# A state product in three rounded products, with the step size moved into an exponent

## The chip, the cores and the metric

The kernel runs on one core of a Trainium2 chip. A core has a matrix engine (TensorE, in the profile PE, with its weight loads as PEld), a vector engine (VectorE, DVE), an engine for functions of one variable (ScalarE, ACT), a general one (GpSimd, POOL) and a queue that issues transfers (SyncE, SP). TensorE reads SBUF and writes PSUM, a small memory of eight banks. DVE and ACT reach both; POOL and the transfers reach SBUF only. The metric is the device time of one execution in microseconds (us).

## The reference, cut to what matters

The kernel computes one layer of a decoder: a pooling branch and a state-space branch (SSD) run on the same 1024 prompt rows and 64 sample rows, are gated, added and projected. The change lies in the SSD of the prompt rows, which go in 8 chunks of 128 rows, for 4 groups of 8 heads (head width 64, state width 128):

```python
acs = jnp.cumsum(dq * Ag, axis=1)
seg = acs[:, :, None] - acs[:, None, :]
decay = jnp.exp(jnp.where(mask, seg, -jnp.inf))
cb = jnp.einsum('bign,bjgn->bijg', Cq, Bq)
att = cb[..., None] * decay * dq[:, None]
y = jnp.einsum('bijge,bjgep->bigep', att, xq)
y = y + jnp.einsum('bign,bige,bgepn->bigep', Cq, jnp.exp(acs), h)
last = acs[:, -1]
w_in = jnp.exp(last[:, None] - acs) * dq
h = h * jnp.exp(last)[..., None, None] + jnp.einsum('bjgn,bjge,bjgep->bgepn', Bq, w_in, xq)
```

Here `dq` is dt, the step size of each row and head. It enters twice: in `att`, which weights the rows of x inside a chunk, and in `w_in`, which weights them on their way into the state `h` that goes from chunk to chunk.

## The kernel before

The kernel is written as Python generators that a scheduler turns into one instruction stream for each engine. Its order of engines' work comes from the order in the program and from a simulated timeline. In the chunk stage the order on PE and on SP is fixed to that of the program (`ORDER`, L1838, applied by `in_line`, L1873); on ACT, DVE and POOL the scheduler chooses it beforehand, and each engine then takes its instructions strictly one after another.

Products in fp32 run in the full type, or split: a matrix is rounded to the shorter type F32R (`hi`), the rest is kept (`lo`), and three products hi·hi, lo·hi and hi·lo are added in PSUM. The large matrices (`gemm_`, L353, line L358) are done so.

Before the chunk stage, `dt_end` (from L1082) makes for all chunks dt (`dtT`), the cumulated decays (`acT`), the weights into the state (`wdT`) and a copy of the decays in DRAM (`acs_d`), from which each chunk loads its own, spread over the partitions.

The chunk stage runs 32 generators `chunk(g, c)` (L1495), 8 chunks in each of 4 groups, staggered in a loop (L1849 to L1868). One of them goes through these steps:

- A: loads of the decays `dec`, of B and C (`bc`) and of x (`xb`);
- B: `cE` = exp(-decay) on ACT; then `far` on POOL (L1198) masks the upper half of `dec`, and `exps` (L1207) makes eight exponentials on ACT, one for each head, with `acT` as bias;
- C: PE transposes x to `px` (L1516) and B to `pbc` (L1518) and makes C·B beside it (L1519). ACT copies the transposed B out (`bt`, L1521) and C in (L1523). DVE makes `xd` = x·dt (L1527) and `xw` = x·w_in (L1529), both out of `px`, and multiplies `dec` and `cE` (L1534, L1536);
- D: PE makes the state product `pu` (L1541), one product in full fp32 of 128 by 128 by 512, and the inner products (`inner`, L1219 and L1222); POOL and DVE update the state `hst` (L1547, L1549), DVE adds the skip term (L1554);
- E: `finish` (L1474 to L1485) gates, splits and squares the result; after the last chunk of a group PE turns the state for its output (L1561).

In iteration i of the loop stand step C of chunk i+1, then filler, then D of chunk i, the loads and exponentials of chunks i+3 and i+2, E of chunk i, and filler again. The filler (`products`, L1831) are pieces of the large projections, 2.56 of them for a chunk, each 12 products of 352 or 384 columns (L358); DVE or ACT takes each out (L1732, L1750, L1753). From chunk 10 on, `wo_splits` (L1779) also splits a weight matrix with work for DVE, ACT, POOL and both transfer queues.

`px`, `pbc`, the output of `inner` and the turned state are PSUM tiles of one kind, `ps` (`PB`, L97), four banks in turn. `pu` has one bank of its own (`PC`), the filler three (`PA`). `bt` and `xd` have two buffers, `xw` has one.

Of the kernel before, what the change touches and what calls it, by code (L numbers as in the profile page):

```python
# [8 lines left out]
F32 = mybir.dt.float32  # L9
F32R = mybir.dt.float32r  # L10
AF = mybir.ActivationFunctionType
ALU = mybir.AluOpType
# [8 lines left out]
P = 128  # L21
# [7 lines left out]
NH = 32  # L29
# [4 lines left out]
NC = SEQ // CH  # L34
# [12 lines left out]
def tile_pool_ssd_step(  # L47
# [9 lines left out]
    def nm(s):  # L57
        uid[0] += 1
        return f"{s}_{uid[0]}"
# [3 lines left out]
    sm = ctx.enter_context(tc.tile_pool(name="sm", bufs=2))  # L63
# [6 lines left out]
    def open_(name, bufs, side="left"):  # L70
        cm = tc.tile_pool(name=name, bufs=bufs, side=side, reuse_waits="tile")
        kept.append(cm)
        return cm.__enter__()
# [20 lines left out]
    def Y4(pool, dt=F32R):  # L94
        return pool.tile([P, 4, T], dt, tag="Y", name=nm("Y"), bufs=2)

    def PB():  # L97
        return psB.tile([P, 512], F32, tag="ps", name=nm("ps"))

    def PA():  # L100
        return psA.tile([P, 512], F32, tag="mm", name=nm("mm"))

    def PC():

        return psC.tile([P, 512], F32, tag="pc", name=nm("pc"))
# [6 lines left out]
    mm = nc.tensor.matmul  # L112
    act = nc.scalar.activation
    V = nc.vector
# [967 lines left out]
    def dt_end():  # L1082
# [87 lines left out]
        for c0 in range(0, 9, 4):  # L1170
# [10 lines left out]
            else:  # L1181
# [2 lines left out]
                act(E[:, :NS], at[:, :NS], AF.Exp, scale=-1.0)  # L1184
                store_(E_d, E[:, :NS])


    SSTEPS = 7

    def decays(dec, g, c):  # L1190

        S = P if c < NC else NS
        load(dec, acs_d[c, 8 * g:8 * g + 8, :S].partition_broadcast(S))

    def far(dec, c):

        if c < NC:
            nc.gpsimd.affine_select(dec, dec, [[0, 8], [1, P]], ALU.is_ge, FAR, base=0, channel_multiplier=-1)  # L1198
        else:
            dS = dec.rearrange("p h (b i) -> p h b i", i=8)  # L1200
            nc.gpsimd.affine_select(dS, dS, [[0, 8], [8, NB], [1, 8]], ALU.is_ge, FAR, base=0, channel_multiplier=-1)
            nc.gpsimd.affine_select(dS, dS, [[0, 8], [-8, NB], [0, 8]], ALU.is_ge, FAR, base=0, channel_multiplier=1)

    def exps(dec, g, c):
        S = P if c < NC else NS
        for h in range(8):
            act(dec[:, h], dec[:, h], AF.Exp, bias=acT[:S, c, 8 * g + h:8 * g + h + 1], scale=-1.0)  # L1207
# [6 lines left out]
    def inner(xd, dec, S, state=None, cE=None):  # L1214
        pi = PB()
        for q in range(4):
            o = [pi[64 * hh:64 * hh + 64, q * S:(q + 1) * S] for hh in range(2)]
            for hh in range(2):
                mm(o[hh], xd[:S, 2 * q + hh, :], dec[:S, 2 * q + hh], start=True, stop=state is None)  # L1219
            for hh in range(2 if state is not None else 0):  # L1220
                h = 2 * q + hh
                mm(o[hh], state[:, h * 64:h * 64 + 64], cE[:, h], start=False, stop=True)  # L1222
        return pi[:, :4 * S].rearrange("p (q i) -> p q i", i=S)
# [242 lines left out]

    CKL = ("sz", "v")

    def ckt(shape, tag, bufs=2):
        return (cl if tag in CKL else ca if tag in ("dec", "xb", "cE", "bc") else ck).tile(list(shape), F32, tag=tag, name=nm(tag), bufs=bufs)  # L1470

    def finish(g, o, S, v, sz):

        V.tensor_tensor(v, v, sz, ALU.mult)  # L1474
        yhc = yh[g][:, :, o:o + S]
        act(yhc, v, AF.Copy)  # L1476
        act(sz, v, AF.Square)
        nc.gpsimd.tensor_tensor(yl[g][:, :, o:o + S], v, yhc.bitcast(F32), ALU.subtract)  # L1478
        nc.gpsimd.tensor_tensor(sz[:, 0:2], sz[:, 0:2], sz[:, 2:4], ALU.add)
        sa = sq_acc[:, o:o + S]  # L1480
        if g == 0:
            nc.gpsimd.tensor_tensor(sa, sz[:, 0], sz[:, 1], ALU.add)
        else:
            nc.gpsimd.tensor_tensor(sz[:, 0], sz[:, 0], sz[:, 1], ALU.add)
            nc.gpsimd.tensor_tensor(sa, sa, sz[:, 0], ALU.add)  # L1485

    def sample_end(g):
        sz = ckt([P, 4, NS], "szs", 1)
        load(sz, z_d[g][:, :, SEQ:])
        v = ckt([P, 4, NS], "v", 1)  # L1490
        load(v, ys_d[g])
        yield
        finish(g, SEQ, NS, v, sz)

    def chunk(g, c):  # L1495
        o = c * P
        dec = ckt([P, 8, P], "dec", 3)
        decays(dec, g, c)
        bc = ckt([P, 2, P], "bc", 3)
        load(bc, xbc_d[g][:, 4:6, o:o + P])  # L1500
        Bf, Cf = bc[:, 0], bc[:, 1]
        xb = ckt([P, 4, P], "xb", 5)
        load(xb, xbc_d[g][:, 0:4, o:o + P])
        yield
        if c > 0:
            cE = ckt([P, 8, P], "cE")
            act(cE, dec, AF.Exp, scale=-1.0)
        if g > 0 or c > 0:
            far(dec, c)
            exps(dec, g, c)  # L1510
            yield
        sz = ckt([P, 4, P], "sz", 3)
        load(sz, z_d[g][:, :, o:o + P])
        px = PB()
        for q in range(4):
            nc.tensor.transpose(px[:, q * P:(q + 1) * P], xb[:, q], ident)  # L1516
        pbc = PB()
        nc.tensor.transpose(pbc[:, :P], Bf, ident)  # L1518
        mm(pbc[:, P:2 * P], Bf, Cf, start=True, stop=True)  # L1519
        bt = ckt([P, P], "bt", 2)  # L1520
        act(bt, pbc[:, :P], AF.Copy)  # L1521
        if c > 0:
            act(pbc[:, 2 * P:3 * P], Cf, AF.Copy)  # L1523
        pxv = px.rearrange("p (h d) -> p h d", d=64)
        heads = slice(8 * g, 8 * g + 8)
        xd = ckt([P, 8, 64], "xd", 2)
        V.tensor_tensor(xd, pxv, dtT[:, c, heads].unsqueeze(2).to_broadcast([P, 8, 64]), ALU.mult)  # L1527
        xw = ckt([P, 8, 64], "xw", 1)
        V.tensor_tensor(xw, pxv, wdT[:, c, heads].unsqueeze(2).to_broadcast([P, 8, 64]), ALU.mult)  # L1529
        if g == c == 0:  # L1530
            yield
            far(dec, c)
            exps(dec, g, c)
        V.tensor_tensor(dec, dec, pbc[:, P:2 * P].unsqueeze(1).to_broadcast([P, 8, P]), ALU.mult)  # L1534
        if c > 0:
            V.tensor_tensor(cE, cE, pbc[:, 2 * P:3 * P].unsqueeze(1).to_broadcast([P, 8, P]), ALU.mult)  # L1536
        yield
        if c == 0:
            yh[g], yl[g] = [Y4(hs if g % 2 else hp) for _ in range(2)]
        pu = PC()  # L1540
        mm(pu, bt, xw.rearrange("p h d -> p (h d)"), start=True, stop=True)  # L1541
        pi = inner(xd, dec, P, *((hst[g], cE) if c > 0 else ()))
        hn = ckt([P, 512], "hst", 2)
        if c == 0:
            act(hn, pu, AF.Copy)
        else:
            nc.gpsimd.tensor_tensor(hn.rearrange("p (h d) -> p h d", d=64), hst[g].rearrange("p (h d) -> p h d", d=64),  # L1547
                                    Elb[:, c, heads].unsqueeze(2).to_broadcast([P, 8, 64]), ALU.mult)
            V.tensor_tensor(hn, hn, pu, ALU.add)  # L1549
        hst[g] = hn  # L1550

        v = xb
        for q in range(4):
            V.scalar_tensor_tensor(v[:, q], v[:, q], Dv[:, 4 * g + q:4 * g + q + 1], pi[:, q], ALU.mult, ALU.add)  # L1554
        yield
        finish(g, o, P, v, sz)
        if c == NC - 1:
            yield
            pt = PB()
            for q in range(4):  # L1560
                nc.tensor.transpose(pt[:, q * P:(q + 1) * P], hn[:, q * P:(q + 1) * P], ident)  # L1561
            fo = ckt([P, 4, P], "xb", 5)
            act(fo, pt.rearrange("p (q n) -> p q n", n=P), AF.Copy)
            store_(new_ssm_p[0, 0, 8 * g:8 * g + 8].rearrange("(q h) p n -> (h p) q n", h=2), fo)
# [129 lines left out]
    def to_chunks():  # L1694
        nonlocal right, ca
        right.__exit__(None, None, None)
        right = tc.tile_pool(name="ca", bufs=3, side="right", reuse_waits="tile")
        ca = right.__enter__()
        right_all.append(right)
        seq.extend(chunk(g, c) for g in range(NG) for c in range(NC))  # L1700
        next(seq[0])
    first_ws, first_g = {}, []
    ca = None
# [13 lines left out]
    cl = open_("cl", 2)  # L1717
    right = tc.tile_pool(name="ck", bufs=2, side="right", reuse_waits="tile")
    ck = right.__enter__()
# [324 lines left out]
    px, py, pz = PA(), PA(), PA()  # L2044
# [57 lines left out]
    for half in range(2):  # L2102
        c = slice(half * 512, half * 512 + 512)
# [124 lines left out]
```

## Time and profile before

| what | value |
|---|---|
| median of 3 runs | 1267.1 us (1266.44 to 1268.58) |
| span of the profiled execution | 1265.2 us |
| its time with what lies around the span | not shown apart; the span is 1.9 us below the median |
| granted TensorE clock | 0.999 |
| busy in the span: PE, DVE, POOL, ACT | 1239.8, 974.4, 716.2, 682.6 us |
| chunk stage | 807 to 1099 us |
| busy in the chunk stage: PE, DVE, POOL, ACT | 288.7, 235.7, 188.8, 180.6 us of 292 |

A group of instructions stands in one row: line, engine, operation, what is written and read (with shapes), how often; then its busy time, the mean time of one, and the idle time of its engine just before, with what ended it. A row of the timeline has its start, its length, and in brackets the idle time before it. Lengths of products overlap, since PE starts one while the one before still drains; the distance between starts is the time that one costs.

### The profile page before, as it was taken

To read this page: it belongs to the slowest core of one execution; us is meant where nothing else is said; L and a number is where in the kernel's file an instruction comes from. 1 tells how busy PE (TensorE), PEld (TensorE's weight loads), DVE (VectorE), ACT (ScalarE), POOL (GpSimd) and SP (SyncE) were. 2 spreads that over 40 slices of the span, in tenths; PEclk is the share of its full clock that TensorE was granted. 3 is DMA by queue.
4 is the path that set the end of the run, shared out by engine and by line. 5 is a ranking of instruction groups with operands and counts; after the bars stand their busy time and mean duration, and the time that the engine had idled before them with its cause. 6 is when DMAs were issued, how large, how long until landed. Compare 5 with 4: busy or idle time off the path is not lost.

```text
span 1265.2 us, 26432 instructions
## 1 busy us (share of the span) xinstructions
PE 1239.8 (98%) x9679; PEld 1158.1 (92%) x9679; DVE 974.4 (77%) x1713; ACT 682.6 (54%) x1566; POOL 716.2 (57%) x607
## 2 busy tenths in 40 slices
PE   7999999999999999999999999999999999999997
PEld 6779999999999999999999989998888988999886
DVE  4686689986998598876676775488677988759986
ACT  4665347465556546455656554646676656401425
POOL 1006767886968777764444444354686877503662
PEclk9999999999999999999999999999999999999999
DMA  9836554564546545444666565998878887866884
GB/s 328 265 112 205 152 158 155 180 205 157 162 154 199 160 155 176 131 150 122 175 177 194 166 178 154 324 308 274 253 241 288 279 250 247 275 226 219 250 192 158
DMA packets 262499, 257.99 MB, mean 204 GB/s; under 512 B 29761, under 2 KB 200337, under 8 KB 262362
## 3 DMA queue, kind: packets, MB, share of 16 engines
q1 hardware_dynamic: 181632, 163.93, 42.7%
q10 hardware_dynamic: 78434, 88.18, 20.2%
q0 software_dynamic: 2304, 4.20, 1.8%
q8 instruction: 77, 1.26, 0.4%
q14 instruction: 52, 0.43, 0.1%
HBM read 171.26 MB, written 85.10 MB: 203 GB/s over the span
## 4 chain that ended last, share of the span: by engine, by line
PE 65%; DMA 2%; DVE 2%; ACT 1%; issue 1%; POOL 0%; SPq 0%; ACTq 0%; DVEq 0%
PE mm L358 17%; PE mm L614 14%; PE ps L614 14%; PE ps L1219 3%; PE pc L614 2%; PE pc L1541 2%; PE ps L1222 2%; PE ps L2023 2%; PE ps L2025 2%; PE ps L2024 2%; PE ps L1309 1%; PE ps L1516 1%; PE ps L1332 1%; PE pc L1323 1%; PE mm L2033 1%
## 5 line engine op out<-in xcount | busy, mean ns | idle before, releaser
L168 POOL TENSOR_TENSOR wlo<-rawA,whi 128x512 fp32r<-128x512 f32 x120 | 174.2, 1456 | 175.2 <-ACT whi L165 89.8
L168 POOL TENSOR_TENSOR wlo<-raw,whi 128x512 fp32r<-128x512 f32 x92 | 153.2, 1674 | 106.9 <-ACT whi L165 75.3
L358 PE MATMUL mm<-Y,whi 128*128 128x352 f32 (+1 forms) x960 | 196.2, 334 | 0.3 <-DVE Y L1579 0.3
L358 PEld LDWEIGHTS mm<-Y,whi 128*128 128x128 f32 x960 | 159.1, 188 | 6.6 <-issue 5.1
L1062 DVE SCALAR_TENSOR_TENSOR GA<-GA,cvT,GA 128x1112 f32<-128x1112 f32 x72 | 133.4, 1857 | 0.1
L614 PE MATMUL mm<-Y,whi 128*128 128x272 f32 x832 | 125.3, 292 | 1.5 <-DVE Y L484 1.1
L614 PE MATMUL ps<-Y,whi 128*128 128x272 f32 x832 | 122.4, 289 | 0.0
L165 ACT ACTIVATE whi<-rawA 128x512 fp32r<-128x512 f32 x125 | 78.1, 627 | 76.0 <-PE ps L614 42.1
L165 ACT ACTIVATE whi<-raw 128x512 fp32r<-128x512 f32 x96 | 59.4, 628 | 106.4 <-DVE raw L546 48.4
L614 PEld LDWEIGHTS mm<-Y,whi 128*128 128x128 f32 x832 | 112.1, 188 | 4.8 <-DVE Y L484 1.5
L614 PEld LDWEIGHTS ps<-Y,whi 128*128 128x128 f32 x832 | 110.9, 188 | 0.4
L1207 ACT ACTIVATE dec<-dec,acT 128x128 f32<-128x128 f32 (+1 forms) x288 | 86.9, 383 | 27.0 <-POOL dec L1198 26.4
L358 PE MATMUL mm<-Y,wlo 128*128 128x352 f32 (+1 forms) x480 | 98.7, 327 | 0.0
L358 PEld LDWEIGHTS mm<-Y,wlo 128*128 128x128 f32 x480 | 81.7, 188 | 0.0
L434 POOL TENSOR_TENSOR pw<-pw,ph 128x512 fp32r<-128x512 f32 x40 | 68.4, 1711 | 12.6 <-ACT ph L432 11.5
L614 PE MATMUL mm<-G,whi 128*128 128x272 f32 x496 | 73.4, 289 | 0.0
L614 PE MATMUL ps<-G,whi 128*128 128x272 f32 x496 | 72.6, 288 | 0.0
L614 PE MATMUL mm<-Y,wlo 128*128 128x272 f32 x416 | 69.3, 288 | 0.0
L614 PE MATMUL ps<-Y,wlo 128*128 128x272 f32 x416 | 69.2, 288 | 0.0
L614 PEld LDWEIGHTS mm<-G,whi 128*128 128x128 f32 x496 | 66.6, 189 | 0.7
L614 PEld LDWEIGHTS ps<-G,whi 128*128 128x128 f32 x496 | 66.3, 188 | 0.0
L1478 POOL TENSOR_TENSOR Y<-xb,Y 128x512 fp32r<-128x512 f32 x32 | 41.7, 1304 | 37.0 <-ACT Y L1476 37.0
(531 smaller groups left out, 3192.5 us busy)
## 6 DMA issues: line engine op xcount, KB each, us to landing
rawA<-in_w_in SPq DMA_DIRECT2D x62, 512.0 KB
dec<-acs_d SPq DMA_DIRECT2D x32, 512.0 KB
xbc<-GA ACTq DMA_DIRECT2D x24, 512.0 KB
Y<-wo SPq DMA_DIRECT2D x10, 1024.0 KB
pw<-in_w_ssm_out ACTq DMA_DIRECT2D x32, 256.0 KB
ws<-ph ACTq DMA_DIRECT2D x32, 256.0 KB
ws<-pw ACTq DMA_DIRECT2D x32, 256.0 KB
h<-in_state_ssm SPq DMA_DIRECT2D x32, 256.0 KB
```

The source lines that it names most:

```text
L165: ins = act(hi[:, :, :ncols], raw[:, :, :ncols], AF.Copy)
L168: (eng or nc.gpsimd).tensor_tensor(lo[:, :, :ncols], raw[:, :, :ncols], hi[:, :, :ncols].bitcast(F32), ALU.subtract)
L358: mm(ps[:, :n], w[k // 4][h][:, k % 4, :], r[k][:, o:o + n], start=(j == 0), stop=(j == len(terms) - 1))
L434: nc.gpsimd.tensor_tensor(raw.bitcast(F32R), raw, hi.bitcast(F32), ALU.subtract)
L614: mm(p, w[j // 8][:, k], A(k, s)[j // 4 == 1], start=(j == 0), stop=(j == 11))
L1062: V.scalar_tensor_tensor(d[:, :n], rp[:, k:k + n], cvT[:, 24 * k + mc:24 * k + mc + 1], d[:, :n], ALU.mult, ALU.add)
L1207: act(dec[:, h], dec[:, h], AF.Exp, bias=acT[:S, c, 8 * g + h:8 * g + h + 1], scale=-1.0)
L1219: mm(o[hh], xd[:S, 2 * q + hh, :], dec[:S, 2 * q + hh], start=True, stop=state is None)
L1222: mm(o[hh], state[:, h * 64:h * 64 + 64], cE[:, h], start=False, stop=True)
L1478: nc.gpsimd.tensor_tensor(yl[g][:, :, o:o + S], v, yhc.bitcast(F32), ALU.subtract)
L1541: mm(pu, bt, xw.rearrange("p h d -> p (h d)"), start=True, stop=True)
L2023: mm(ps, hi, y[:, k, c0:c0 + cw], start=(first and k == 0), stop=False)
```

## The change

The change has four parts.

1. `dt_end` adds ln(dt) to `acT` of the prompt's chunks, after the cumulated decays have been sent to DRAM. As `acT` is the bias of the exponentials in `exps`, `dec` then holds decay·dt, and x needs no weighting for the inner products.
2. `xd` is therefore a plain copy of `px`, made by ACT where DVE multiplied.
3. DVE weights `px` in place, in PSUM, with `wdT`. The product is split from there: ACT rounds it to `xh`, DVE subtracts to get `xl`. Both have one buffer.
4. The transposed B is split as well: ACT's copy now rounds (`bh`), DVE subtracts (`bl`, in a buffer of another pool with four of them). The state product becomes three products in F32R: bh·xh, bl·xh, bh·xl.

```diff
+        ld = sp.tile([P, 512], F32, tag="xd", name=nm("ld"), bufs=2)[:, :NC * NH]
+        V.tensor_scalar(ld, dtT[:, :NC].rearrange("p c h -> p (c h)"), 1e-37, None, ALU.max)
+        act(ld, ld, AF.Ln)
+        V.tensor_tensor(acT[:, :NC].rearrange("p c h -> p (c h)"), acT[:, :NC].rearrange("p c h -> p (c h)"), ld, ALU.add)
...
-        bt = ckt([P, P], "bt", 2)
-        act(bt, pbc[:, :P], AF.Copy)
+        bh = ckt([P, P], "bt", 2, F32R)
+        bl = sm.tile([P, P], F32R, tag="stc", name=nm("bl"), bufs=4)
+        act(bh, pbc[:, :P], AF.Copy)
         if c > 0:
             act(pbc[:, 2 * P:3 * P], Cf, AF.Copy)
...
-        V.tensor_tensor(xd, pxv, dtT[:, c, heads].unsqueeze(2).to_broadcast([P, 8, 64]), ALU.mult)
-        xw = ckt([P, 8, 64], "xw", 1)
-        V.tensor_tensor(xw, pxv, wdT[:, c, heads].unsqueeze(2).to_broadcast([P, 8, 64]), ALU.mult)
+        act(xd, pxv, AF.Copy)
+        V.tensor_tensor(pxv, pxv, wdT[:, c, heads].unsqueeze(2).to_broadcast([P, 8, 64]), ALU.mult)
+        xh, xl = ckt([P, 512], "xw", 1, F32R), ckt([P, 512], "xwl", 1, F32R)
+        act(xh, px, AF.Copy)
+        V.tensor_tensor(bl, pbc[:, :P], bh.bitcast(F32), ALU.subtract)
...
         if c > 0:
             V.tensor_tensor(cE, cE, pbc[:, 2 * P:3 * P].unsqueeze(1).to_broadcast([P, 8, P]), ALU.mult)
+        V.tensor_tensor(xl, px, xh.bitcast(F32), ALU.subtract)
         yield
...
-        mm(pu, bt, xw.rearrange("p h d -> p (h d)"), start=True, stop=True)
+        mm(pu, bh, xh, start=True, stop=False)
+        mm(pu, bl, xh, start=False, stop=False)
+        mm(pu, bh, xl, start=False, stop=True)
```

The helper `ckt` gets a type as a further argument for this.

More of the change, by code (lines that the diff above doesn't have):

```diff
@@ L1467, in tile_pool_ssd_step, with ckt @@
     CKL = ("sz", "v")
-    def ckt(shape, tag, bufs=2):
-        return (cl if tag in CKL else ca if tag in ("dec", "xb", "cE", "bc") else ck).tile(list(shape), F32, tag=tag, name=nm(tag), bufs=bufs)
+    def ckt(shape, tag, bufs=2, dt=F32):
+        return (cl if tag in CKL else ca if tag in ("dec", "xb", "cE", "bc") else ck).tile(list(shape), dt, tag=tag, name=nm(tag), bufs=bufs)
     def finish(g, o, S, v, sz):
```

## The prediction

> **What bounds the kernel now.** I read the page first, then the busy times by stretch, the chain of waits, and at last the groups and the timelines of the chunk stage.
>
> ```profile
> span 1265.2 us, 26432 instructions
> ...
> PE 1239.8 (98%) x9679; PEld 1158.1 (92%) x9679; DVE 974.4 (77%) x1713; ACT 682.6 (54%) x1566; POOL 716.2 (57%) x607
> ```
>
> TensorE (PE) is busy for 98% of the span. The change works in the chunk stage, from 807 to 1099 us: 32 chunks, so 292/32 = 9.1 us for one. Busy time there by stretch (columns: length, PE, PEld, DVE, ACT, POOL, clock, DMA share, GB/s):
>
> ```profile
> 900.00:950.00 50.00, 50.00 (x419) 45.01 (x419) 37.98 (x63) 36.12 (x96) 36.55 (x40) 1.00 0.81 248
> ...
> 1000.00:1050.00 50.00, 48.49 (x383) 42.45 (x383) 43.26 (x75) 30.19 (x80) 33.47 (x38) 1.00 0.86 272
> 1050.00:1099.00 49.00, 47.41 (x395) 42.22 (x392) 41.94 (x74) 25.62 (x65) 36.92 (x40) 1.00 0.82 269
> sum 292.00, PE 288.65 PEld 256.92 DVE 235.69 ACT 180.62 POOL 188.80; mean PE 48.11 PEld 42.82 DVE 39.28 ACT 30.10 POOL 31.47
> ```
>
> PE misses only 3.35 of 292 us, all of it in the last 99 us. There DVE idles just 99 - 85.2 = 13.8 us. So a PE saving counts in full until DVE, or a hand-over between ACT and DVE, is late. The chain of waits over one late chunk (start, length, what):
>
> ```profile
> 1074.73 0.44 PE ps L1516 x4
> ...
> 1075.50 1.93 PE mm L358 x12
> 1077.43 0.86 PE pc L1541 x2
> ...
> 1080.18 2.12 PE mm L358 x12
> 1082.30 0.44 PE ps L1516 x4
> 1082.74 0.11 PE ps L1518
> ```
>
> It is PE throughout: transposes of chunk i+1 (L1516, L1518), filler products (L358), the state product of chunk i (L1541), its inner products, filler, the next transposes. The wait that PE already suffers here, from the view of waits:
>
> ```profile
> PE ps L1518 <- DVE xw L1529: 2.3, 2, 1.6
> ```
>
> It is the key to this change. Tiles named ps turn over four banks. A chunk takes them in the order px(i+1), pbc(i+1), pi(i), so the bank of px(i+1) goes to pbc(i+2). The transpose at L1518 cannot start before the last reader of the previous chunk's px has finished. That reader is now xw, one DVE instruction.
>
> **The change, part by part.**
>
> *State product.* One full fp32 product (two PE records) becomes three F32R products of 512 columns. On PE's timeline, the fp32 one, and F32R products of that width in the tail:
>
> ```profile
> 959.20 1.02 PE L1541 MATMUL pc<-xw,bt 128*128 128x512 f32 x2
> 960.15 1.09 PE L1219 MATMUL ps<-dec,xd 128*64 128x128 f32 x16
> ...
> 1144.78 0.40 PE L2024 MATMUL pc<-Y,a11h 128*128 128x512 f32 x1
> 1145.02 0.40 PE L2023 MATMUL ps<-Y,a11h 128*128 128x512 f32 x1
> 1145.25 0.39 PE L2024 MATMUL ps<-Y,a11h 128*128 128x512 f32 x1
> ```
>
> The fp32 product holds PE for 960.15 - 959.20 = 0.95 us, of which 0.86 is its own (chain row) and 0.09 the switch to the half-width weights of L1219. F32R products start every (1145.25 - 1144.78)/2 = 0.235 us, so three take 0.70; with the same switch, 0.79. Saving 0.16 us, 32 times: -5.1 us. Ends: without the switch 0.25 x 32 = -8.0; if the three do not overlap at all and each holds PE for its whole 0.40, 3 x 0.40 = 1.20 against 0.95, +8.0. I take -5.1, since the tail has the same shape and type. The Trainium skill ("FP8 and Floating Point Precision", TensorE Precision Notes) counts true FP32 as four passes; three products for four passes would save a quarter of the 0.86, an estimate of -6.9 us by that page. The trace has 0.86/0.235 = 3.7.
>
> *DVE.* Groups of the chunk stage (busy, mean ns | idle before), then by line the nearest shapes for the small subtraction and for a multiply from PSUM to PSUM:
>
> ```profile
> L1534 DVE TENSOR_TENSOR dec<-dec,ps 128x1024 f32<-128x1024 f32 x32 | 38.9, 1217 | 19.5 <-ACT ps L1523 8.8 <-POOL sz L1484 2.5 <-POOL Y L1478 2.3
> ...
> L1529 DVE TENSOR_TENSOR xw<-ps,wdT 128x512 f32<-128x512 f32 x32 | 21.8, 681 | 4.1 <-PE pc L1541 4.1
> L1527 DVE TENSOR_TENSOR xd<-ps,dtT 128x512 f32<-128x512 f32 x32 | 21.8, 681 | 6.0 <-PE ps L1516 6.0
> ```
> ```profile
> L1292 DVE TENSOR_TENSOR bt<-ps,bt x8: 283/283/283, 604.9 to 765.6; 32x128 fp32r<-32x128 f32 x8
> ```
> ```profile
> L2119 DVE TENSOR_TENSOR ps<-ps,half x11: 423/699/700, 1223.7 to 1257.9; 128x512 f32<-128x512 f32 x9, 128x256 f32<-128x256 f32 x2
> ```
>
> Gone: xd and xw, 2 x 0.68 = 1.36. New: the weighting in place 0.70, xl 0.68, bl 0.28, together 1.66. DVE gains 0.30 us a chunk, 9.6 in all. I charge 0, as its 56 idle us (292 - 236) cover it; the thin cover in the last 99 us is a rival below.
>
> *ACT.* Nearest rows for the two new copies (from PSUM; rounding to F32R):
>
> ```profile
> L1476 ACT ACTIVATE Y<-xb 128x512 fp32r<-128x512 f32 x32 | 19.8, 622 | 20.5 <-DVE xb L1474 20.5
> ...
> L1545 ACT ACTIVATE hst<-pc 128x512 f32<-128x512 f32 x4 | 2.4, 592 | 1.4 <-PE pc L1541 0.9 <-ACT xb L1563 0.5
> ```
>
> Two copies, 0.59 + 0.62 = 1.21 us a chunk, 38.7 in all; ACT goes from 181 to 219 of 292 us busy. As load this is covered and costs 0. Its place is what counts. Where xh waits on ACT, the exponentials (cE, eight for dec) and the output stores on ACT's queue stand behind it, and POOL's masking waits for cE. SP's and POOL's own queues get nothing new.
>
> *The release of px.* Before: the transposes, then xd and xw on DVE. After: xd copy (ACT), weighting (DVE), xh (ACT; one buffer, so it also waits until the state product of the chunk before has read the old one), xl (DVE). Four hops over two engines, where both earlier ones lay on one. What slack is there? The end of xw against the start of L1518, in the five tightest chunks (DVE's timeline, then PE's):
>
> ```profile
> 920.94 0.68 DVE L1529 TENSOR_TENSOR xw<-ps,wdT 128x512 f32<-128x512 f32 x1
> ...
> 1017.72 0.68 DVE L1529 TENSOR_TENSOR xw<-ps,wdT 128x512 f32<-128x512 f32 x1
> ...
> 1035.15 0.68 DVE L1529 TENSOR_TENSOR xw<-ps,wdT 128x512 f32<-128x512 f32 x1
> ...
> 1064.57 0.68 DVE L1529 TENSOR_TENSOR xw<-ps,wdT 128x512 f32<-128x512 f32 x1
> ...
> 1080.51 0.67 DVE L1529 TENSOR_TENSOR xw<-ps,wdT 128x512 f32<-128x512 f32 x1
> ```
> ```profile
> 921.76 0.27 PE L1518 MATMUL ps<-ident,bc 128*128 128x128 f32 x1
> ...
> 1018.46 0.33 PE L1518 MATMUL ps<-ident,bc 128*128 128x128 f32 x1 [0.74 <-DVE xw L1529]
> ...
> 1036.53 0.27 PE L1518 MATMUL ps<-ident,bc 128*128 128x128 f32 x1
> ...
> 1065.30 0.33 PE L1518 MATMUL ps<-ident,bc 128*128 128x128 f32 x1 [1.59 <-DVE xw L1529]
> ...
> 1082.58 0.27 PE L1518 MATMUL ps<-ident,bc 128*128 128x128 f32 x1
> ```
>
> The slack is 0.14, 0.06, 0.70, 0.05 and 1.40 us. How much later will the release be? On ACT in the last of these chunks:
>
> ```profile
> 1079.75 0.26 ACT L1521 ACTIVATE bt<-ps 128x128 f32<-128x128 f32 x1
> 1079.91 2.44 ACT L1207 ACTIVATE dec<-dec,acT 128x128 f32<-128x128 f32 x8
> 1082.25 0.26 ACT L1523 ACTIVATE ps<-bc 128x128 f32<-128x128 f32 x1
> ```
>
> ACT gets to this chunk's first copy only at 1079.75, 4.6 us after its transposes (1075.17 in the chain), and then runs eight exponentials for 2.44 us. The xd copy comes after L1521. At best it ends near 1080.6, weighting 1081.3, xh 1081.9, xl 1082.6: just at the deadline. With the exponentials in between, it is 2.4 late. I take as added delay both ACT copies and half such a block: 0.59 + 0.62 + 1.22 = 2.43 us, an estimate: with ACT busy 219 of 292 us, a hop meets such a block about as often as not. Less the slack, the five chunks lose 2.29 + 2.37 + 1.73 + 2.38 + 1.03 = 9.8 us. Ends: only xh is added and runs at once (0.62): 0.48 + 0.56 + 0.57 = 1.6; the whole block stands ahead (3.65): 15.9.
>
> *Once.* A maximum, a logarithm and an addition where the decays are made:
>
> ```profile
> 594.24 1.28 ACT L1184 ACT_TABLE_LOAD   x1 [2.11 <-DVE u L623]
> ```
> ```profile
> 585.00:615.00 30.00, 30.00 (x250) 29.00 (x249) 16.61 (x33) 22.70 (x48) 16.19 (x13) 1.00 0.53 150
> ```
>
> At most two more table loads and a copy-sized logarithm, 2 x 1.28 + 0.6 = 3.2 us on ACT, while PE never stops and ACT has 7.3 idle of 30: I charge 0, 3.2 if uncovered. The bias of the exponentials keeps its place and count; bh takes bt's.
>
> Sum: -5.1 + 9.8 = +4.7. The profiled span of 1265.2 becomes 1269.9. It stands 1.9 below the median of the runs, which includes what lies around the span; so 1267.1 + 4.7 = 1271.8 us.
>
> **The rivals.**
>
> *Faster: the extra hops stay hidden.* The added delay is the 0.62 of xh alone: -5.1 + 1.6 = -3.5, 1263.6 us. For it: PE loses only 2.3 us at this wait today, and the order on ACT and DVE is made anew for the changed kernel, so the tight places need not be the same. Against it: ACT's late start above. The balance tips at an added delay of 1.5 us, where the five chunks lose 1.36 + 1.44 + 0.80 + 1.45 + 0.10 = 5.1.
>
> *No change: DVE is the bound in the late part.* If its 13.8 idle us there are waits that stay, the last 11 chunks stretch by 11 x 0.30 = 3.3 and lose their PE saving (11 x 0.16 = 1.8): -5.1 + 1.8 + 3.3 = 0, so 1267.1 us. Against it: some of that idle time must be free to use.
>
> *Slower by PE itself: weights are not loaded beside the product before.* Then 3 x 0.40 counts, +8.0, 1275.1 us, and with the stalls above 1284.9. Against it: the 0.235 between starts in the tail, where each product also has a weight load. The Trainium skill ("TensorE: Matmul & The Clock Gate", Part 3, What overlaps and what doesn't) lets a weight load overlap a running product only in another row group, which would forbid it here; the tail's rows contradict that.
>
> **How the numbers follow.** Forecast 0.46, hidden hops 0.35, DVE-bound 0.14, no overlap 0.05. About 0.2% (2.5 us) is what this kernel's measurement can tell. So faster 0.35, same 0.14, slower 0.51. The forecast's own range is 1268 (delay near 2 us) to 1278 (15.9 lost: 1267.1 - 5.1 + 15.9). The whole range runs from 1260, near the -8.0 end (1259.1), to 1280, between 1278 and the 1284.9 of the last rival.
>
> **What would show it.** L1541's successors: about 0.79 us from the first of the three products to the first L1219; 1.2 would mean no overlap. DVE busy in the stage near 245 us, ACT near 219. The view of waits should name the transpose of B waiting for xl on DVE, for some 10 us instead of 2.3, with xl in turn waiting for xh on ACT. The forecast is wrong if that wait stays near 2 us, or if PE waits rather for products' evacuations or for dec.

## The result and the profile after

| | before | after |
|---|---|---|
| median of the runs compared | 1267.76 us (1266.44 to 1268.58) | 1278.65 us (1277.12 to 1280.92) |
| ratio, 95% interval | | 1.0086 [1.0064, 1.0107] |
| span of the profiled execution | 1265.2 us | 1275.4 us |
| chunk stage, first transpose of x to last turned state | 807.5 to 1099.1: 291.6 us | 809.3 to 1109.1: 299.8 us |
| rest of the span behind it | 166 us | 166 us |

The kernel became slower by 10.9 us, where 4.7 were forecast. In the later series of runs the kernel before had medians of 1268.5 to 1271.6 us and went up to 1277.4 us, with a granted clock between 0.999 and 0.993, so the sign of the 10.9 us is safer than its size.

Line numbers of the changed kernel: x transposes L1521, B's transpose L1523, C·B L1524, the copies `bh` L1527 and `xd` L1533, weighting L1534, `xh` L1536, `bl` L1537, `dec` L1542, `cE` L1544, `xl` L1545, the three products L1550 to L1552, inner products L1224 and L1227, the weight split on DVE L1815 to L1820. In the profile `xh` and `xl` are named xw and xwl, `bh` is bt.

The first lines of the page after:

```profile
span 1275.4 us, 26603 instructions
...
PE 1240.3 (97%) x9711; PEld 1168.6 (92%) x9711; DVE 978.7 (77%) x1747; ACT 715.0 (56%) x1632; POOL 712.7 (56%) x607
```

PE is busy as long as before (1239.8), with cheaper products: it waits more, and part of its work runs at a lower clock. Busy time by stretch in the chunk stage (columns as in the prediction: length, PE, PEld, DVE, ACT, POOL, clock, DMA share, GB/s):

```profile
850.00:900.00 50.00, 50.00 (x400) 46.76 (x398) 39.04 (x75) 36.09 (x94) 27.02 (x31) 1.00 0.87 282
900.00:950.00 50.00, 45.82 (x384) 42.23 (x384) 37.49 (x60) 36.42 (x93) 35.30 (x40) 0.93 0.71 218
...
sum 300.00, PE 287.84 PEld 266.28 DVE 239.90 ACT 211.68 POOL 186.59; mean PE 47.97 PEld 44.38 DVE 39.98 ACT 35.28 POOL 31.10
```

From 850 to 900 us PE misses nothing; from there on it misses 4.18 us in the first 50 alone, and the clock falls below 1. What PE waited for, over the chunk stage (us in total, times, longest):

```profile
PE ps L1523 <- DVE cE L1544: 6.2, 3, 4.2
PE ps L1523 <- DMA xb<-xbc: 2.1, 1, 2.1
PE ps L1523 <- ACT xd L1533: 1.9, 1, 1.9
PE ps L1523 <- issue: 1.8, 1, 1.8
```

Together these are 12.0 us, against 2.3 before, and all stand before one instruction, the transpose of B. Elsewhere in the stage PE waits 0.3 us, against 1.0 before. The view names what came last by the profile; what really ended these waits is worked out below. PE's timeline shows what the product costs now, and the longest of these waits with what follows it (last column: x how many):

```profile
907.03 0.39 PE L1550 MATMUL pc<-xw,bt 128*128 128x512 f32 x1
907.25 0.40 PE L1551 MATMUL pc<-xw,bl 128*128 128x512 f32 x1
907.49 0.39 PE L1552 MATMUL pc<-xwl,bt 128*128 128x512 f32 x1
907.81 0.44 PE L1224 MATMUL ps<-dec,xd 128*64 128x128 f32 x4
...
920.57 0.81 PE L358 MATMUL mm<-Y,whi 128*128 128x352 f32 x4
921.21 0.60 PE L1521 MATMUL ps<-ident,xb 128*128 128x128 f32 x4
925.99 0.45 PE L1523 MATMUL ps<-ident,bc 128*128 128x128 f32 x1 [4.18 <-DVE cE L1544]
...
926.52 1.52 PE L358 MATMUL mm<-Y,whi 128*128 128x352 f32 x4
```

From the first product to the first inner product it is 907.81 - 907.03 = 0.78 us, against 0.95 before. The wait of 4.18 us ends with `cE`, and behind it the same four filler products take 1.52 us instead of 0.81. The granted clock in that stretch, and in one after another wait (2.09 us, at 1073.7):

```profile
1074.20:1077.40 3.20, 3.20 (x14) 3.20 (x13) 3.20 (x6) 1.82 (x4) 3.20 (x5) 0.53 0.78 299
...
926.50:931.00 4.50, 4.50 (x16) 4.35 (x16) 4.50 (x9) 2.62 (x7) 4.08 (x5) 0.50 0.49 146
```

In finer windows, the clock is 0.50 from 924.3 to 931.0 and from 1074.5 to 1077.8 us, and 1.00 on both sides of each. PE worked from 926.0 on in the first, so it ran some 5.1 and 3.4 us at half its clock, which cost (5.1 + 3.4) x 0.5 = 4.25 us.

So the 8.2 us by which the stage grew come out of three terms: the product 32 x (0.79 - 0.95) = -5.1, the waits 12.3 - 3.3 = +9.0 (of which +9.7 at the transpose of B), the half clock +4.25; their sum is +8.15. The remaining 1.8 us of the span arise ahead of the stage. There the clock is 0.50 from 736.5 to 739.9 us, behind a wait of 1.76 us; the kernel before waits 1.73 us at the same place and keeps 1.00. They are not put down to the change: a variant below that has all of it (the weight split off DVE) enters the stage at 807.0.

Why is `cE` so late at 921? DVE's timeline after, and the one row of before that answers to it:

```profile
918.79 1.24 DVE L1815 TENSOR_TENSOR R<-R,R 128x512 f32<-128x512 f32 x1 [2.37 <-DMA R<-in_w_o]
...
921.16 1.53 DVE L1819 TENSOR_TENSOR R<-R,R 128x512 f32<-128x512 f32 x1
922.61 0.68 DVE L1534 TENSOR_TENSOR ps<-ps,wdT 128x512 f32<-128x512 f32 x1
923.21 0.27 DVE L1537 TENSOR_TENSOR bl<-ps,bt 128x128 fp32r<-128x128 f32 x1
923.41 1.20 DVE L1542 TENSOR_TENSOR dec<-dec,ps 128x1024 f32<-128x1024 f32 x1
924.53 1.21 DVE L1544 TENSOR_TENSOR cE<-cE,ps 128x1024 f32<-128x1024 f32 x1
...
928.00 0.68 DVE L1545 TENSOR_TENSOR xwl<-ps,xw 128x512 fp32r<-128x512 f32 x1
```
```profile
923.26 1.21 DVE L1536 TENSOR_TENSOR cE<-cE,ps 128x1024 f32<-128x1024 f32 x1
```

DVE stands 2.37 us for a transfer of the weight split, with the chunk's work queued behind, and makes up for it until 925.7. Before, the same stop lasted 3.81 us and `cE` ended at 924.5, but PE passed at 921.76: there its transpose needed only `xw`, done at 921.6. The two programs give out the four ps banks differently. By the addresses in the programs, which the traces do not hold, `pbc` took over a bank of a `px` in 20 of 30 cases before, and in 2 of 30 after; in 22 it took the bank of the `pbc` before it, whose last reader is `cE`. The banks do not go round in fixed turn. That the scheduler hands out the one that it plans to be free first, now that `px` is held until `xl`, is the likely reason and was not tested.

The trace agrees with this where PE waits. Six transposes of B wait longer than 0.5 us. Five of them start 0.06 to 0.26 us behind the end of the previous chunk's `cE`, whatever the view names; the sixth, in chunk 25 of the 32, starts 0.10 us behind DVE's skip term (L1565), the last reader of the inner products' bank. In all six the previous chunk's `xl` ends later still, by 0.3 to 3.0 us: at 928.68 in the first, where PE went on at 925.99. So in this order of DVE a bank of `px` would have come later, not sooner.

The groups of the new instructions in the chunk stage (busy, mean ns | idle time before):

```profile
L1534 DVE TENSOR_TENSOR ps<-ps,wdT 128x512 f32<-128x512 f32 x32 | 22.1, 692 | 14.3 <-ACT xd L1533 14.2
L1545 DVE TENSOR_TENSOR xwl<-ps,xw 128x512 fp32r<-128x512 f32 x32 | 21.8, 681 | 0.1
...
L1536 ACT ACTIVATE xw<-ps 128x512 fp32r<-128x512 f32 x32 | 18.8, 588 | 6.2 <-PE pc L1551 4.1 <-DVE ps L1534 2.0
L1533 ACT ACTIVATE xd<-ps 128x512 f32<-128x512 f32 x32 | 18.8, 586 | 9.1 <-PE ps L1521 9.1
```

DVE stops 14.3 us in all for the copy of `xd`, which the weighting in place must let pass. `xl` hardly ever stops for `xh` (0.1).

### The profile page after: what moved, and what is told of

Its sections match the earlier page's. It is cut to its first block, busy times and chain, and to the rows that moved or that the text cites. A ratio compares the mean times of both kernels' runs of the same rounds, so it can differ in the third digit from the quotient of the medians.

```text
span 1275.4 us, 26603 instructions
## 1 busy us (share of the span) xinstructions
PE 1240.3 (97%) x9711; PEld 1168.6 (92%) x9711; DVE 978.7 (77%) x1747; ACT 715.0 (56%) x1632; POOL 712.7 (56%) x607
## 4 chain that ended last, share of the span: by engine, by line
PE 64%; DVE 3%; DMA 2%; ACT 2%; issue 1%; SPq 0%; ACTq 0%; POOL 0%; DVEq 0%
PE mm L358 16%; PE mm L614 14%; PE ps L614 13%; PE ps L1224 2%; PE pc L614 2%; PE ps L1227 2%; PE ps L2034 2%; PE ps L2036 2%; PE ps L2035 2%; PE ps L1314 1%; DMA dec<-acs_d 1%; PE ps L1521 1%; PE ps L1337 1%; PE pc L1328 1%; PE mm L2044 1%
```

## The experiments

Three explanations were weighed. *Bank*: PE waits because the transposed B gets a bank that is freed late; in the right bank the loss goes. *Chain*: the way of x over ACT, DVE, ACT, DVE to `xl` is too long by itself, whatever the bank. *DVE as a whole*: in the last 200 us it is late with everything, since it works strictly in order and the weight split stands among the chunks' work. The texts written ahead of the runs call these theories A, B and C, in this order; in the first of them, B takes in all of the added work on ACT and DVE.

**The three products alone.** The kernel before, with three F32R products of the same two rounded operands; the low parts are left out, so DVE and ACT do nothing new.

```diff
-        bt = ckt([P, P], "bt", 2)
+        bt = ckt([P, P], "bt", 2, F32R)
...
-        xw = ckt([P, 8, 64], "xw", 1)
+        xw = ckt([P, 8, 64], "xw", 1, F32R)
...
-        mm(pu, bt, xw.rearrange("p h d -> p (h d)"), start=True, stop=True)
+        for j in range(3):
+            mm(pu, bt, xw.rearrange("p h d -> p (h d)"), start=j == 0, stop=j == 2)
```

> The kernel before with the state product as three F32R products, nothing else of the change; the two low parts are left out (both operands are rounded on their way into SBUF, and the same pair is multiplied three times), so only the time of the product is measured. Theory A (the change lost its time at the bank that the transposes of B take): the banks are passed on as before, so the time falls by the PE saving alone, 32 x 0.16 us, to 1262 to 1264 us; first product to first inner product 0.79 us; wait at the transposes of B still 2 to 3 us. Theory B (it lost it to the extra copies on ACT and the longer DVE work): the same here, since neither is added. Rival (the three products do not overlap): slower by about 8 us.

Measured: 0.9962 [0.9942, 0.9982], some 4.8 us faster. PE's timeline and waits:

```profile
903.29 0.86 PE L1542 MATMUL pc<-xw,bt 128*128 128x512 f32 x3
904.08 0.44 PE L1219 MATMUL ps<-dec,xd 128*64 128x128 f32 x4
```
```profile
PE ps L1518 <- DVE xw L1529: 2.2, 2, 1.2
PE ps L1219 <- DVE cE L1536: 1.3, 2, 0.8
```

The product costs 904.08 - 903.29 = 0.79 us, and the saving reaches the end time, by the interval 2.3 to 7.4 us of it. The waits at the transpose of B stay at 2.2 us; 1.3 us are new at the inner products, for `cE`.

**The logarithm and the copy alone.** The kernel before, with ln(dt) in the bias (the four lines of the change, left out here) and `xd` copied by ACT.

```diff
...
-        V.tensor_tensor(xd, pxv, dtT[:, c, heads].unsqueeze(2).to_broadcast([P, 8, 64]), ALU.mult)
+        act(xd, pxv, AF.Copy)
```

> The kernel before with the logarithm of dt in the exponent and xd as a copy by ACT; the state product stays one fp32 product and xw is weighted by DVE as before. DVE loses 0.68 us a chunk, ACT gains 0.59. Theory A: px is still released by xw and C's bank passed on as before, so the time is within 3 us of before, 1264 to 1270. Theory B: the copy standing late on ACT holds px; the waits at the transposes of B grow and name ACT's copy, 1270 us or more.

Measured: 1.001 [0.9987, 1.0033], no difference; B's transposes wait 2.8 us for `xw`, starting 0.05 to 0.10 us behind its end, as before. Neither the logarithm nor one more copy on ACT costs time by itself.

**The kernel before with one fixed bank for the transposed B.** No computation is changed; `pbc` always follows `pbc`, and `px` and the inner products have three banks.

```diff
+    pin = []
...
-        pbc = PB()
+        if not pin:
+            pin.append(PB())
+        pbc = pin[0]
```

> The kernel before, only with pbc of all chunks in one fixed bank, so that the transpose of B always waits for the multiplication of cE of the chunk before, as in 22 of 30 chunks of the changed kernel; px and the inner products have three banks. Theory A: the wait at the transposes of B grows to 8 us or more and the kernel becomes 5 to 15 us slower, without any of the change's copies or products. Theory B: no more than 2 us slower.

Measured: 1.0104 [1.0055, 1.0153]. Waits and timeline (the transpose of B is L1521 here, those of x L1517):

```profile
PE ps L1521 <- ACT cE L1508: 6.6, 3, 3.8
PE ps L1521 <- ACT ph L1787: 2.2, 1, 2.2
PE ps L1521 <- issue: 2.1, 1, 2.1
```
```profile
1025.59 0.60 PE L1517 MATMUL ps<-ident,xb 128*128 128x128 f32 x4
1030.03 0.45 PE L1521 MATMUL ps<-ident,bc 128*128 128x128 f32 x1 [3.84 <-ACT cE L1508]
...
1030.56 1.63 PE L358 MATMUL mm<-Y,whi 128*128 128x384 f32 x4
```

The view names ACT here, but each of the five stops over 0.5 us ends 0.10 us behind DVE's multiplied `cE` (L1539). Handing `pbc`'s bank to the next `pbc` costs the old kernel, without any of the change, about as much as the whole change does, with waits for the same reader and the same slow products behind them. So this order of the banks is enough for the loss. That another order would have spared the changed kernel does not follow from it.

**The changed kernel with two fixed banks for it, in turn.**

```diff
+    pin = []
...
-        pbc = PB()
+        if len(pin) < 2:
+            pin.append(PB())
+        pbc = pin[c % 2]
```

> The changed kernel with pbc alternating between two fixed banks, so that the transpose of B waits for the chunk before the last; px and the inner products share the two other banks. Theory A: the waits at the transposes of B vanish and the time falls from 1278 to 1263 to 1268 us, unless the transposes of x now wait for the inner products' bank. Theory B: it stays above 1273 us, with PE waiting elsewhere for ACT or DVE.

Measured: 1.012 [1.0082, 1.0157]. B's transposes wait no more, but the two banks that are left are short:

```profile
PE ps L1522 <- issue: 8.3, 4, 3.2
PE ps L1224 <- ACT xb L1577: 5.6, 3, 2.7
```

L1522 are the transposes of x. The wait has moved, not gone.

**Weighted x in SBUF.** `px` is released by the weighting, two hops earlier; the weight split's `ph` gives up a buffer to make room.

```diff
-        V.tensor_tensor(pxv, pxv, wdT[:, c, heads].unsqueeze(2).to_broadcast([P, 8, 64]), ALU.mult)
-        xh, xl = ckt([P, 512], "xw", 1, F32R), ckt([P, 512], "xwl", 1, F32R)
+        xh, xl, xw = ckt([P, 512], "xw", 1, F32R), ckt([P, 512], "xwl", 1, F32R), ckt([P, 512], "xwf", 1)
+        V.tensor_tensor(xw.rearrange("p (h d) -> p h d", d=64), pxv, wdT[:, c, heads].unsqueeze(2).to_broadcast([P, 8, 64]), ALU.mult)
-        act(xh, px, AF.Copy)
+        act(xh, xw, AF.Copy)
...
-        V.tensor_tensor(xl, px, xh.bitcast(F32), ALU.subtract)
+        V.tensor_tensor(xl, xw, xh.bitcast(F32), ALU.subtract)
...
-            hi = ck.tile([P, 512], F32R, tag="ph", name=nm("ph"), bufs=3)
+            hi = ck.tile([P, 512], F32R, tag="ph", name=nm("ph"), bufs=2)
```

> The changed kernel, but DVE writes the weighted x into SBUF and both parts of it are split from there, so px is released by that one multiplication, as by xw before; to make room, the split of the late weight matrix has two buffers in place of three. The load of ACT and DVE is that of the changed kernel. In 24 of 30 chunks the transposes of B take the bank of px again. Theory A (bank): waits at the transposes of B fall from 13 to 2 to 4 us, and the time is 1 to 6 us below before. Theory B (load and hops on ACT and DVE): still 5 to 11 us above before.

Measured: 1.0077 [1.0047, 1.0106]. By the addresses, `pbc` takes a bank of `px` again in 24 of 30 cases, and B's transposes wait 2.4 us. But:

```profile
PE pc L1552 <- DVE xwl L1545: 6.6, 3, 2.6
PE ps L1523 <- issue: 2.4, 1, 2.4
```

PE now stops at the third product, for `xl`. The bank was not the whole story: with it out of the way, the chain to `xl` is late at the same places. The three stops stand at the products of chunks 13, 24 and 29, which follow the transposes of 14, 25 and 30.

**The same with `xl` on POOL.** One line of it differs:

```diff
-        V.tensor_tensor(xl, xw, xh.bitcast(F32), ALU.subtract)
+        nc.gpsimd.tensor_tensor(xl, xw, xh.bitcast(F32), ALU.subtract)
```

> As the run with the weighted x in SBUF, with the subtraction that makes the low part on POOL in place of DVE (1.3 us a chunk there, 0.68 off DVE). Theory A: 2 to 6 us below before. Theory B: with DVE lighter than before by 0.4 us a chunk it is between before and 5 us above it. If POOL is too late with it, PE waits at the third product.

Measured: 1.0022 [1.0001, 1.0043], the lowest ratio of the changed kernels, and still no gain:

```profile
PE pc L1552 <- POOL xwl L1545: 6.4, 5, 2.2
```

**The inner products' output in a bank of the filler's**, which leaves the four ps banks to `px`, `pbc` and the turned state; in the changed kernel, and in the kernel before as a control.

```diff
-    def inner(xd, dec, S, state=None, cE=None):
-        pi = PB()
+    def inner(xd, dec, S, state=None, cE=None, bank=PB):
+        pi = bank()
...
-        pi = inner(xd, dec, P, *((hst[g], cE) if c > 0 else ()))
+        pi = inner(xd, dec, P, *((hst[g], cE) if c > 0 else (None, None)), PA)
```

> The changed kernel with the output of the inner products in one of the three banks of the filler, so that px and pbc have four banks for themselves; load and order of the copies are untouched. In 25 of 30 chunks the transposes of B wait for the px of the chunk before the last. Theory A: the waits at the transposes of B go, and the time is 0 to 5 us below before, unless the filler now waits for its banks. Theory B: still 5 us or more above before.

> The control for that: the kernel before with the same move of the inner products' output. Both theories: within 3 us of before, its 2.7 us of waits at the transposes of B gone, some new waits of the filler.

Measured: 1.0062 [1.004, 1.0084] and, for the control, 1.001 [0.9995, 1.0024]. In the changed kernel:

```profile
PE pc L1552 <- DVE xwl L1545: 6.2, 3, 2.7
PE mm L358 <- DVE G L1764: 2.4, 2, 1.8
```

No transpose of B waits any more, and again 6.2 us stand at the third product, in chunks 13, 24 and 29; the filler, which gave up a bank, waits 2.4 us. Two different ways to take the bank out of it leave the same wait for `xl`.

**The third product last.** If `xl` alone were late, it should be enough to use it later. The line moves behind the inner products, which take 1.9 us; in the changed kernel and in both SBUF variants.

```diff
-        mm(pu, bh, xl, start=False, stop=True)
         pi = inner(xd, dec, P, *((hst[g], cE) if c > 0 else ()))
+        mm(pu, bh, xl, start=False, stop=True)
```

> The changed kernel with the third product (bh times xl) moved behind the inner products of the same chunk on PE, nothing else. The inner products take about 1.9 us on PE, so xl may come 1.9 us later before PE stops for it. Theory A (the wait sits where the bank of the transposed B is handed over): xl is not what PE waits for in the changed kernel, so the move alone leaves 10 to 13 us of waits at the transposes, and the ratio to the kernel before stays at 1.006 to 1.011. Theory B (all added waits come from the chain to xl being late): the six waits shrink by up to 1.9 us each, and the ratio comes near 1.000.

> The variant with the weighted x in SBUF and xl on DVE (px released early, 1.0077), with the third product moved behind the inner products, some 1.9 us later on PE. There PE lost 6.6 us in three waits (longest 2.6) at the third product. Theory B (the chain to xl is too late by itself): of these waits some 0.5 to 1.5 us remain, the slow products behind them go too, the stage gets 6 to 8 us shorter, and the ratio comes to 1.001 to 1.003. Theory C (what is late is DVE as a whole in these places, so that PE only meets it at the next thing that it needs from DVE, the multiplied dec or cE): the waits turn up at the inner products instead, and the ratio stays at 1.006 to 1.009.

> The variant with the weighted x in SBUF and xl on POOL (1.0022; PE lost 6.4 us in five waits at the third product, longest 2.2), with the third product moved behind the inner products, some 1.9 us later on PE. Theory B (the chain to xl is too late by itself): at most 0.5 us of these waits remain, and with the slow products behind them 6 to 8 us go: ratio 0.996 to 0.998, faster than the kernel before by more than the measurement's uncertainty, and the saving of the three products (4 to 5 us) shows at last. Theory C (DVE late as a whole): waits at the inner products for dec or cE instead, ratio 1.000 to 1.003.

Measured: 1.0039 [1.0019, 1.006], 1.0063 [1.004, 1.0086] and 1.0071 [1.0044, 1.0097]. The waits, in this order:

```profile
PE ps L1523 <- DVE cE L1544: 6.7, 3, 3.5
PE ps L1523 <- DMA wo<-ph: 2.4, 1, 2.4
PE ps L1523 <- DMA xb<-xbc: 1.7, 1, 1.7
```
```profile
PE pc L1550 <- DVE hst L1560: 8.2, 3, 4.3
PE pc L1550 <- ACT ps L1529: 2.9, 1, 2.9
PE pc L1550 <- ACT ph L1795: 1.5, 1, 1.5
```
```profile
PE pc L1550 <- DVE hst L1560: 7.5, 3, 3.8
```

In the changed kernel the move leaves 10.8 us at B's transposes, as expected if the bank is waited for; the ratio is lower than expected (1.006 to 1.011), and why is open. In the SBUF variants nothing stops for `xl` any more, and PE stops one step further on: the next chunk's first product wants the bank of `pu`, which DVE's addition to the state (L1560) has not read yet. Each of these stops, also where the view names ACT, ends 0.15 us behind that addition. Moving the product was also no favour to it, since `pu` is finished later, so the test is not a clean one. Still, that only the chain to `xl` is late no longer fits: whatever of DVE's work PE asks for next is late.

**The weight split off DVE.** The changed kernel, with its 16 additions and subtractions on POOL.

```diff
-    WOE = V
+    WOE = nc.gpsimd
```

> The changed kernel with the 16 additions and subtractions of the weight split (R, 128 by 512 each) moved from DVE to POOL; nothing in the chunks is changed. Theory C (DVE is late as a whole in the last 200 us of the chunk stage, because it takes its instructions in order and the weight split stands among the chunk's own, waiting for transfers for up to 2.4 us at a time): DVE gets some 16 x 0.9 = 14 us of work and its waits for these transfers less, the waits of the transposes of B fall from 10 to 13 us to under 4, the slow products behind them go, and the ratio to the kernel before is 0.996 to 1.000. Theory B (the chain through ACT and DVE to xl and to the multiplied cE is too late by its own hops): the waits stay at 8 us or more and the ratio at 1.005 to 1.010. In between, about 1.003: both. POOL gets about 16 x 1.28 = 20 us more, from 142 of the last 200 us to some 162; if POOL becomes late instead, the waits name its masking or the state's scaling.

Measured: 1.0096 [1.007, 1.0121]. The waits of PE, and of SP's queue in this kernel and in the changed one (from 895 us on):

```profile
PE ps L1521 <- DMA xb<-xbc: 10.1, 3, 5.7
PE ps L1224 <- DVE dec L1542: 0.9, 1, 0.9
PE ps L1523 <- ACT xd L1533: 0.8, 1, 0.8
```
```profile
SPq L1518 <- POOL sq_acc L1490: 48.9, 7, 15.1
```
```profile
SPq L1518 <- POOL sq_acc L1490: 30.2, 8, 6.6
```

Half of the expectation came true. B's transposes wait 1.0 us in all instead of 12.0, although 22 of 30 `pbc` still follow a `pbc`. The first of them, in chunk 14, comes ahead of any stop for x. There `cE` ends at 919.5 instead of 925.7, and the transpose waits 0.39 us instead of 4.35 (counted as in the table below): it was the weight split, standing in DVE's order, that made `cE` late. The later ones show it less purely, since the stops for x give DVE time as well. The time is not won, because POOL falls behind with the squares, the load of z on SP's queue waits for POOL (48.9 us instead of 30.2), and the loads of x queue behind it; PE stops up to 5.7 us for one. That was not among the places where I had looked for a late POOL.

No version with the whole change in it ran faster than the kernel before.

## Why the prediction was right, and where it was not

Forecast 1271.8 us, slower with a chance of 0.51; measured 1278.65. The sign and the place of the loss hold, the size was 4.7 against 10.9.

- *State product, -5.1*: right, 0.79 us as worked out, and with the products alone 4.8 us of it arrive at the end. In the changed kernel the mean is 0.82, since two chunks' products fall into stretches of half clock (1.19 and 1.07 us). The rival without overlap of weight loads is refuted: three products with their loads fit into 0.79 us, so the trace again goes against the rule of the Trainium skill ("TensorE: Matmul & The Clock Gate", Part 3, What overlaps and what doesn't) that was weighed there.
- *DVE*: the new instructions last 0.69, 0.68 and 0.28 us, as taken. Busy in the stage 239.9 us, not 245. The no-change rival, DVE at its limit, is not what happened: from 900 to 1100 us it is busy 163.1 us, less than before (165.5). It is late without being full. Charging its load at nothing was right for the load and missed the order: 2 to 4 us behind a transfer are passed on to all that follows.
- *ACT*: the copies last 0.59 us each; 211.7 us busy, not 219. On both engines neighbouring rows overlap by some 0.1 us (a copy of 0.58 us at 917.03 on ACT is followed at 917.51), so added work adds less busy time than its lengths sum to; whether that is all of the difference was not traced. `xl` was to stop for `xh`; it is the weighting that stops for `xd` (14.3 us).
- *The release of px, +9.8*: the waits grew by 9.7 us, at the instruction and in the chunks named, but not for the reason given. Between the start of x's last transpose and that of B's, less the usual 0.11 us, PE waited as follows (the start of x's last transpose in each kernel; the forecast is of the growth):

| chunk of the 32 | before | after | growth | forecast |
|---|---|---|---|---|
| 14 | 921.65: 0.00 | 921.54: 4.35 | 4.35 | 2.29 |
| 21 | 982.86: 0.00 | 988.24: 2.01 | 2.01 | none |
| 25 | 1017.45: 0.90 | 1024.25: 1.92 | 1.02 | 2.37 |
| 27 | 1036.42: 0.00 | 1043.14: 1.57 | 1.57 | 1.73 |
| 30 | 1063.44: 1.75 | 1071.32: 2.25 | 0.50 | 2.38 |
| 32 | 1082.47: 0.00 | 1092.04: 0.78 | 0.78 | 1.03 |

  All five tight chunks wait, and one more. The bank waited for, though, is mostly that of the previous `pbc`, with `cE` as its last reader, not that of `px` with `xl`. The step that failed is the rule that the bank of px(i+1) always goes to pbc(i+2): the scheduler makes the order of the banks anew for each program. The chunks were right because those where `xw` was just in time are those where DVE is late; in four of the five, all but 27, `cE` came behind `xw` there already before. That the sum fits is in part luck: had the rule held in this order of DVE, the six transposes would have waited for `xl`, 0.3 to 3.0 us longer each, and others besides. The chain to `xl` is the second limit, which showed (6.2 to 6.6 us) once the bank was out of the way.
- *Left out*: the half clock behind some of the waits, +4.25 us in the stage. In the chunk stage of before, the clock stays at 1.00, and the longest wait that the view names is 1.6 us. With this term, the forecast of the stage would have been +8.95 against 8.2.
- *Two small slips of the working*: of the 3.35 us that PE misses in the stage before, 3.1 lie in the last 99 us, not all. And the lower end of the forecast's own range, 1268, belongs to an added delay of 1.7 us; one of 2 us gives 1269.7.
- *Once, 0*: right. With the logarithm alone the time does not change.
- *The rival of hidden hops*, 0.35, argued that the order is made anew. It was, but the tight places stayed, and the waits went to another bank instead of away.

What stays open: which of the new hops (weighting in place, `xh`, `bl`, `xl`) takes how much of the slack, since the split was never run without the logarithm; and whether an order of DVE exists in which the weight split meets no chunk. Four of the six stops lie within 12 us behind the starts of DVE's four blocks of the weight split (918.8, 976.6, 1020.4 and 1067.3 us), those of chunks 27 and 32 some 23 to 25 us behind.

## What to carry to other kernels

A saving on the engine that is always busy arrives whole only if its suppliers keep their times; run it alone first, since the saving and what pays for it can be told apart in one run each. Where an engine takes its instructions in a fixed order, ask what stands behind each of its waits for a transfer, not only what share of the time it is busy. When several fixes each remove the wait that the profile names and the time stays, the named wait is only where a common lateness is met first, and the fix belongs at what is late.

## What the runs showed of the hardware

- *A wait of some 2 us can be paid twice.* In the changed kernel the granted clock was 0.50 in a stretch of 6.7 us around the end of a wait of 4.18 us, and for 3.3 us behind one of 2.09 us and 3.4 us behind one of 1.76 us. After one of 1.85 us, at 990.4, it did not fall: the four products behind it took 0.88 us. Nor did it after 1.73 us at 735.3 in the kernel before. What decides between these is open. The Trainium skill ("TensorE: Matmul & The Clock Gate", Part 1, What's actually happening) has the clock fall to half after an idle window of some 3.4 us, with windows that run freely. The half is what the trace shows; here two waits shorter than that window were enough.
- *Three F32R products of 512 columns cost 0.79 us with the switch to the narrower weights behind them*, in place of 0.95 for the one in fp32. In the rows at 907 us, the three start 0.22 and 0.24 us apart, and the inner product follows the last after 0.32.
